# Gate and up of the last feed-forward part as Strassen products in a two-layer trunk kernel on one Trainium2 core

## The chip, the core and the metric

The kernel runs on one core of a Trainium2 chip. The metric is the device time of one execution in microseconds (us); the time of a kernel is the median of several runs. The core has TensorE (matrix products, PE in the profile; its weight loads are PEld), VectorE (DVE), ScalarE (ACT), GpSimd (POOL), SyncE (SP, which issues most of the loads) and 16 DMA engines. Each engine runs its instructions in a fixed order and waits for the others by semaphores.

## What is computed

Two layers over 640 tokens (128 of a context, 512 latent ones) of width 1024. Each layer adds three parts to the residual stream `h`: a feed-forward part, four parallel head groups, and a second feed-forward part. The second feed-forward part of the second layer, with the final norm behind it, ends the program.

```python
def swiglu(x, wg, wu, wd):                       # widths 1024 -> 2816 -> 1024
    return (jax.nn.silu(x @ wg) * (x @ wu)) @ wd

def trunk_layer(h, cond, p, ctx):
    m = modulation(cond, p["w_mod"], p["b_mod"])
    sh1, sc1, g1, sh2, sc2, g2, sh3, sc3, g3 = [m[:, :, j] for j in range(N_MOD)]
    x = rmsnorm(h, p["norm_ffn1"]) * (1 + sc1) + sh1
    h = h + 0.5 * g1 * swiglu(x, p["ffn1_w_gate"], p["ffn1_w_up"], p["ffn1_w_down"])
    x = rmsnorm(h, p["norm_mix"]) * (1 + sc2) + sh2
    mixed, new_ctx = token_mixing(x, p, ctx)
    h = h + g2 * mixed
    x = rmsnorm(h, p["norm_ffn2"]) * (1 + sc3) + sh3
    h = h + 0.5 * g3 * swiglu(x, p["ffn2_w_gate"], p["ffn2_w_up"], p["ffn2_w_down"])
    return h, new_ctx
```

## The kernel before

**Layout.** Activations lie transposed: 8 blocks of 128 features on the partitions, tokens along the free side, in two halves of 256 and 384 tokens. `hT` holds the residual stream. A product at full precision is three matmuls in a rounded format: each operand is kept as a rounded part and a rest (`xh`, `xl` of the activation, `whi`, `wlo` of the weight), and `mm3` (L270 to L278) issues `whi` by `xh`, `whi` by `xl` and `wlo` by `xh`. The hidden width of 2816 is 22 blocks of 128.

**Weights.** SP loads raw slabs of up to 1 MB into a pool of three (`raw`); a slab of gate or up holds two hidden blocks, 1024 by 256. `prep_to` splits each half of a slab: ACT rounds it (`whi`, L220), DVE subtracts (`wlo`, L221). The pairs lie in a ring of six slots; `w` takes the next one and has the split of the two that follow it written ahead.

**The feed-forward part** (`ffn`) works through the hidden blocks in chunks, here 8, 6 and 8. For each block `gate_up` forms gate and up in PSUM, first for the 256 tokens (one tile `gu` for both), then for the 384, 24 matmuls for each product; then ACT does Silu (`sg`, L724), DVE the product with up (`hx`, L726), ACT rounds it (`hh`, L727), DVE takes the rest (`hl`, L728). In the first chunk the first two blocks (`LEAD`) go together, 256 tokens before 384, with the feature blocks in the outer loop (L713 to L715), so that they can begin while the normalised activations are still being made. After a chunk `res_phase` multiplies its `hh` and `hl` by the down weights (`y`, 8 feature blocks by two halves) and adds each result to `hT` on DVE (L642). In the last chunk the last five feature blocks (`FIN`) go half by half, and the final norm and the output of the 384 tokens run beside the products of the 256.

**The activations** come from `x_prep`: `rb` broadcasts the norm's scale by a matmul (L574), DVE scales (`xt`, L599), ACT adds the shift and rounds (`xh`, L602 or L606 and L608), and the rest `xl` is taken on DVE (L603) or on POOL (L609).

**What sets the order.** The program is written as above, and a scheduler that simulates the engines puts the instructions of each engine in their final order when the kernel is built. `tick` counts off the matmul time written so far and writes side work (norms, `x_prep`) in between when it is due.

Of the kernel before, what the change touches and what calls it, by code (L numbers as in the profile page):

```python
# [33 lines left out]
N_TAB = 2  # L34
T_SUM = 2300
# [79 lines left out]
class Net:  # L115
    def __init__(self, tc, a, depth=DEPTH, dump=None):
# [37 lines left out]
        self.x = [None, None]  # L154

# [48 lines left out]
    def prep_to(self, n):  # L204
        while self.i_prep < min(n, len(self.wq), self.limit):
            sid, f = self.wq[self.i_prep]
            self.load_upto(sid + 1)
            v = f(self.raw[sid])
# [13 lines left out]
            self.ready[self.i_prep] = (hv, lv)  # L222
            self.slab_left[sid] -= 1
# [3 lines left out]
            self.i_prep += 1  # L227

# [298 lines left out]
    def load_x(self):  # L527
# [129 lines left out]
    def ffn_specs(self, l, nm, chunks):  # L657
# [21 lines left out]
    def ffn(self, l, j, nxt, chunks, e_pro=None):  # L679
# [4 lines left out]
        nf = max(n for _, n in chunks[:N_TAB if e_pro else None])  # L684
        for ci, (c0, n) in enumerate(chunks):
# [6 lines left out]
            hh = [hp.tile([P, nf, w], F32R, name=f"hh{i}", tag=f"hh{i}") for i, (_, w) in enumerate(HALVES)]  # L692
            hl = [hp.tile([P, nf, w], F32R, name=f"hl{i}", tag=f"hl{i}") for i, (_, w) in enumerate(HALVES)]

            def gate_up(fs, half, wts):
# [12 lines left out]
                if len(fs) > 1:  # L708
                    for k in range(DB):
                        for i, f in enumerate(fs):  # L710
                            for s in range(2):
# [3 lines left out]
                                nc.tensor.matmul(o, wh[:, k, :], xl[:, k, :], start=False, stop=(k == DB - 1))  # L715
                        self.tick(len(fs) * 6 * (w * 0.417 + 2.5))
# [15 lines left out]
            f = 0  # L732
            while f < n:
# [12 lines left out]
        hps.close()  # L746

# [1207 lines left out]
```

## Time and profile before

| | |
|---|---|
| median of 3 runs | 2568.88 us (2568.11 to 2569.06) |
| the profiled execution | 2565.89 us, of which the profile's span 2564.1 us |
| mean granted clock of TensorE | 0.984 of full speed |
| busy TensorE, share of the span | 97%, 17040 instructions |
| the last feed-forward part | from about 2076 us to the end |
| its largest load | 1 MB per slab of two gate or up blocks |

All rows used come from the profiled execution. The page gives busy times over the whole span; the views by stretch, by line and the timeline show one stretch or one engine of it. In a timeline each line is an instruction or a run of like ones: its start, its length, engine and line of the code, the output tile, the inputs, shapes, how many, and in brackets how long the engine had stood idle and what released it. Lengths of matmuls overlap, since they are pipelined; the distance between two starts is the time that one costs.

### The profile page before, as it was taken

The numbers are of one execution on the slowest core, as the hardware profiler recorded it, in microseconds if no ns is written. First come the engines' busy times: TensorE is split into PE (matmuls) and PEld (weight loads), VectorE is DVE, ScalarE is ACT, GpSimd is POOL, SyncE is SP. The second block draws the span as 40 slices with busy tenths as digits, with TensorE's granted clock in tenths as the row PEclk, the third lists the DMA queues.
The fourth block names the chain that finished last, engine by engine and source line by source line (L and its number), as shares of the span: only waits on it lengthen the run. The fifth ranks groups of instructions, "written<-read, shape, count | busy, mean of one in ns | idle before, by whom it ended". The sixth has DMA issues, their size and how long they took to land.

```text
span 2564.1 us, 41328 instructions
## 1 busy us (share of the span) xinstructions
PE 2485.1 (97%) x17040; PEld 2343.6 (91%) x17040; DVE 1518.8 (59%) x3084; ACT 837.0 (33%) x1620; POOL 322.4 (13%) x453
## 2 busy tenths in 40 slices
PE   7999999999899899999999999999998999999998
PEld 5999999997679899999999999999876799999998
DVE  5767676765778678454356666665567773323333
ACT  5332222242454333222243222223435453222222
POOL 2211111036001111000020000000360010000000
PEclk8999999999899999999999999999999999999999
DMA  8545454430204245333314444441301123222211
GB/s 292 168 125 169 132 168 141 130 116 26 59 9 137 71 128 179 105 115 102 98 42 155 133 144 143 135 144 56 114 12 55 42 91 116 66 71 72 89 50 42
DMA packets 209028, 272.08 MB, mean 106 GB/s; under 512 B 25480, under 2 KB 176232, under 8 KB 208584
## 3 DMA queue, kind: packets, MB, share of 16 engines
q1 hardware_dynamic: 186824, 191.45, 23.5%
q0 software_dynamic: 22016, 78.00, 10.2%
q8 instruction: 134, 2.20, 0.3%
q14 instruction: 54, 0.44, 0.1%
HBM read 254.44 MB, written 14.97 MB: 105 GB/s over the span
## 4 chain that ended last, share of the span: by engine, by line
PE 82%; issue 8%; DVE 5%; DMA 2%; POOL 2%; ACT 1%; SPq 0%; DVEq 0%; POOLq 0%; ACTq 0%
PE gu L276 15%; PE gu L278 14%; PE gu L277 14%; PE y L276 8%; PE y L277 8%; PE y L278 8%; PE pj L1055 1%; PE pj L1056 1%; PE pj L1057 1%; PE gu L713 1%; PE gu L714 1%; PE gu L715 1%; PE macc L460 1%; DMA wf<-in_w_mod_dram 1%; DVE xt L599 1%
## 5 line engine op out<-in xcount | busy, mean ns | idle before, releaser
L276 PE MATMUL gu<-xh,whi 128*128 128x384 f32 (+1 forms) x2560 | 792.8, 310 | 0.8 <-ACT whi L220 0.8
L278 PE MATMUL gu<-xh,wlo 128*128 128x384 f32 (+1 forms) x2560 | 788.4, 308 | 0.9 <-DVE wlo L221 0.9
L277 PE MATMUL gu<-xl,whi 128*128 128x384 f32 (+1 forms) x2560 | 788.4, 308 | 0.0
L220 ACT ACTIVATE whi<-raw 128x1024 fp32r<-128x1024 f32 (+2 forms) x344 | 328.4, 960 | 846.7 <-PE gu L277 429.0
L221 DVE TENSOR_TENSOR wlo<-raw,whi 128x1024 fp32r<-128x1024 f32 (+2 forms) x344 | 377.8, 1101 | 340.8 <-ACT whi L220 339.8
L276 PEld LDWEIGHTS gu<-xh,whi 128*128 128x128 f32 x2560 | 480.3, 188 | 11.8 <-issue 10.0
L277 PEld LDWEIGHTS gu<-xl,whi 128*128 128x128 f32 x2560 | 481.3, 188 | 2.7 <-issue 2.4
L278 PEld LDWEIGHTS gu<-xh,wlo 128*128 128x128 f32 x2560 | 480.6, 188 | 2.2 <-DVE wlo L221 1.3
L276 PE MATMUL y<-hh,whi 128*128 128x384 f32 (+1 forms) x1408 | 437.1, 312 | 0.1
L277 PE MATMUL y<-hl,whi 128*128 128x384 f32 (+1 forms) x1408 | 434.4, 309 | 0.0
L278 PE MATMUL y<-hh,wlo 128*128 128x384 f32 (+1 forms) x1408 | 434.4, 309 | 0.0
L642 DVE SCALAR_TENSOR_TENSOR hT<-y,G,hT 128x128 f32<-128x128 f32 (+1 forms) x432 | 175.5, 435 | 216.7 <-PE y L278 215.9
L411 DVE SCALAR_TENSOR_TENSOR mvec<-wm,cs,mvec 128x512 f32<-128x512 f32 x420 | 294.3, 744 | 10.7 <-DMA wm<-in_w_mod_dram 10.5
L276 PEld LDWEIGHTS y<-hh,whi 128*128 128x128 f32 x1408 | 266.6, 190 | 6.7 <-issue 5.8
L278 PEld LDWEIGHTS y<-hh,wlo 128*128 128x128 f32 x1408 | 266.9, 190 | 0.4 <-issue 0.4
L277 PEld LDWEIGHTS y<-hl,whi 128*128 128x128 f32 x1408 | 267.1, 190 | 0.1
L366 POOL DMA_DIRECT2D wm<-in_w_mod_dram x128 | 92.5, 722 | 1039.3 <-DVE mvec L411 794.8
L726 DVE TENSOR_TENSOR hx<-sg,gu 128x256 f32<-128x256 f32 (+1 forms) x176 | 84.8, 483 | 128.7 <-ACT sg L724 128.6
L727 ACT ACTIVATE hh<-hx 128x256 fp32r<-128x256 f32 (+1 forms) x176 | 82.9, 471 | 171.7 <-DVE hx L726 171.5
L724 ACT ACTIVATE sg<-gu 128x256 f32<-128x256 f32 (+1 forms) x176 | 75.4, 429 | 191.3 <-PE gu L278 188.4
L728 DVE TENSOR_TENSOR hl<-hx,hh 128x256 fp32r<-128x256 f32 (+1 forms) x176 | 86.4, 493 | 63.0 <-ACT hh L727 62.9
L561 POOL TENSOR_TENSOR rst<-ms,mhalf 128x2 f32<-128x2 f32 (+1 forms) x12 | 11.2, 932 | 824.3 <-DVE ms L560 824.3
(340 smaller groups left out, 3205.3 us busy)
## 6 DMA issues: line engine op xcount, KB each, us to landing
wm<-in_w_mod_dram POOLq DMA_DIRECT2D x128, 512.0 KB, 4.1
raw<-in_ffn_w_gate_dram SPq DMA_DIRECT2D x44, 1024.0 KB, 5.4
raw<-in_ffn_w_up_dram SPq DMA_DIRECT2D x44, 1024.0 KB, 5.1
raw<-in_ffn_w_down_dram SPq DMA_DIRECT2D x24, 1024.0 KB, 7.2
raw<-in_ffn_w_down_dram SPq DMA_DIRECT2D x16, 768.0 KB, 4.5
raw<-in_w_in_dram SPq DMA_DIRECT2D x12, 1024.0 KB, 5.4
wf<-in_w_mod_dram SPq DMA_DIRECT2D x8, 1024.0 KB, 12.3
raw<-in_ffn_w_down_dram SPq DMA_DIRECT2D x16, 512.0 KB, 5.2
```

Source lines behind the costliest of these rows:

```text
L220: self.nc.scalar.activation(hv, v, AF.Copy)
L221: self.nc.vector.tensor_tensor(lv, v, hv, op=OP.subtract)
L276: self.nc.tensor.matmul(out, wh, xh, start=(i == 0), stop=False)
L277: self.nc.tensor.matmul(out, wh, xl, start=False, stop=False)
L278: self.nc.tensor.matmul(out, wl, xh, start=False, stop=(i == n - 1))
L366: self.nc.gpsimd.dma_start(out=t.rearrange("p (j c) -> p j c", j=2), in_=w[kk * 256:(kk + 1) * 256, c0:c0 + 512].rearrange("(j p) c -> p j ...
L411: nc.vector.scalar_tensor_tensor(self.mvec[:, v], w, c, self.mvec[:, v], op0=OP.mult, op1=OP.add)
L642: self.pin = nc.vector.scalar_tensor_tensor(h, y[:, s:e], G[:, k, v:v + 1], h, op0=OP.mult, op1=OP.add)
L724: nc.scalar.activation(sg[:, 0:w], g, AF.Silu)
L726: nc.vector.tensor_tensor(hx[:, 0:w], sg[:, 0:w], u, op=OP.mult)
L727: nc.scalar.activation(hh[half][:, f, :], hx[:, 0:w], AF.Copy)
L728: self.pin = nc.vector.tensor_tensor(hl[half][:, f, :], hx[:, 0:w], hh[half][:, f, :], op=OP.subtract)
```

## The change

In the last feed-forward part only, the chunks become 2, 4, 4, 4, 4 and 4 blocks, and from the second chunk on two gate blocks, and then two up blocks, are formed together by a Strassen scheme: the slab's 1024 by 256 weights and the 1024 by 640 activations are each cut in two by two, and seven products of half size (512 by 128 weights, 320 tokens, 12 matmuls) take the place of eight.

- `st_x` forms four combinations of the activations at the start of the part, from `xh` + `xl`, on POOL (20 operations) and DVE, splits them again, and writes one of them over a quarter of `xh` and `xl`. It is written in four steps between the matmuls of the first chunk.
- `st_sums` forms the combinations of a slab's weights by four POOL operations of 128 by 512, three of them in place. Instead of two pieces of 1024 columns, a slab is split in four, `A1`, `S24` and `S3` of 1024 columns and `S1` of 512. The split on ACT and DVE (now L232, L233) stays.
- `st_pair` issues the products into three PSUM regions `a`, `b`, `c` (L852 to L854), partly on top of each other. Partial sums that two results need are copied out by ACT (`copy`) and added by DVE. Silu, `hx`, `hh`, `hl` follow with 320 columns.
- The ring has five slots instead of six, from the second layer's output projection on. `xh`, `xl`, `hh`, `hl` are one tile for all 640 tokens each.
- In the Strassen chunks `res_phase` issues the first two feature blocks of down for all but the chunk's last two hidden blocks first (`early`), and those two behind.

The lines below are those of the change, in the order of the file.

```diff
+CHUNKS_S = ((0, 2), (2, 4), (6, 4), (10, 4), (14, 4), (18, 4))
+RING_S = 5
+S1_BUFS = 1
+W_ST = ("A1", "S24", "S1", "S3")
+TH = NTOK // 2
...
+            if f in W_ST:
+                v = self.st_view(sid, raw, f)
+            else:
+                v = f(raw)
...
+            if f == "A1":
+                self.st_sums(sid, raw)
...
+    def st_view(self, sid, raw, f):
+        if f == "S1":
+            return self.s1.pop(sid)
+        return raw[:, :, P:2 * P] if f == "S3" else raw[:, :, 0:P]
+    def st_sums(self, sid, raw):
+        G = self.nc.gpsimd
+        a11, a12 = raw[:, 0:4, 0:P], raw[:, 4:8, 0:P]
+        a21, a22 = raw[:, 0:4, P:2 * P], raw[:, 4:8, P:2 * P]
+        s1 = self.sx.tile([P, 4, P], F32, name="s1", tag="s1", bufs=S1_BUFS)
+        G.tensor_tensor(s1, a21, a22, op=OP.add)
+        G.tensor_tensor(a21, a11, a21, op=OP.subtract)
+        G.tensor_tensor(a11, s1, a11, op=OP.subtract)
+        G.tensor_tensor(a12, a12, a11, op=OP.subtract)
+        self.s1[sid] = s1
...
+        if not self.xt_free:
+            self.xt = [self.xp.tile([P, DB, NTOK], F32R, name=f"x{c}", tag=f"x{c}") for c in "hl"]
+            self.xt_free = [0, 1]
+        self.xt_free.remove(half)
+        c0, w = HALVES[half]
+        return tuple(t[:, :, c0:c0 + w] for t in self.xt)
...
-                    if f % 2 == 0:
+                    if f >= st:
+                        if f % 2 == 0:
+                            self.add_slab(slab(w, f, 2), W_ST)
+                    elif f % 2 == 0:
...
+        if st < FB:
+            e_sx, self.sx = self.open_pool("sx")
+            tprep = self.st_x()
+        else:
+            tprep = iter(())
...
+                        if half == 1 and k % 2:
+                            next(tprep, None)
...
+            if c0 >= st:
+                for f in range(0, n, 2):
+                    self.st_pair(f, hht, hlt)
+                f = n
...
+            for _ in tprep:
+                pass
             last = ci == len(chunks) - 1
-            self.res_phase(n, [(hh[i], hl[i]) for i in range(2)], [(f, f) for f in range(n)], (l, j), nxt if last else None)
+            self.res_phase(n, [(hh[i], hl[i]) for i in range(2)], [(f, f) for f in range(n)], (l, j), nxt if last else None,
+                           early=(n - 2 if c0 >= st else 0))
...
+        def whole(E, k, c):
+            t = self.t(TH, "tr")[:, 0:TH]
+            E.tensor_tensor(t, xh[:, k, c:c + TH], xl[:, k, c:c + TH], op=OP.add)
+            return t
+        def split(E, t, h, lo):
+            A.activation(h, t, AF.Copy)
+            E.tensor_tensor(lo, t, h, op=OP.subtract)
+        for k in range(4):
+            r12, r11, r22 = whole(V, k, TH), whole(V, k, 0), whole(G, 4 + k, TH)
+            t1 = self.sx.tile([P, TH], F32, name="sg", tag="sg", bufs=4)
+            t1s.append(t1)
+            V.tensor_tensor(t1, r12, r11, op=OP.subtract)
+            G.tensor_tensor(r12, r22, r12, op=OP.subtract)
+            split(G, r12, *(t[:, k, TH:NTOK] for t in self.T23))
+            V.tensor_tensor(r22, r22, t1, op=OP.subtract)
+            split(V, r22, *(t[:, k, 0:TH] for t in self.T23))
+            r21 = whole(G, 4 + k, 0)
+            G.tensor_tensor(r21, r21, r22, op=OP.subtract)
+            split(V, r21, *(t[:, k, :] for t in self.T4))
+            yield
+        for k in range(4):
+            split(V, t1s[k], *(t[:, k, TH:NTOK] for t in self.xt))
...
+        X = {"11": [t[:, 0:4, 0:TH] for t in self.xt], "T1": [t[:, 0:4, TH:NTOK] for t in self.xt],
+             "21": [t[:, 4:8, 0:TH] for t in self.xt], "22": [t[:, 4:8, TH:NTOK] for t in self.xt],
+             "T2": [t[:, :, 0:TH] for t in self.T23], "T3": [t[:, :, TH:NTOK] for t in self.T23], "T4": self.T4}
+        def prod(o, w, k0, x, start):
+            (wh, wl), (bh, bl) = w, X[x]
+            for k in range(4):
+                h, lo = wh[:, k0 + k, :], wl[:, k0 + k, :]
+                nc.tensor.matmul(o, h, bh[:, k, :], start=start and k == 0, stop=False, skip_group_check=True)
+                nc.tensor.matmul(o, h, bl[:, k, :], start=False, stop=False, skip_group_check=True)
+                nc.tensor.matmul(o, lo, bh[:, k, :], start=False, stop=(k == 3), skip_group_check=True)
...
+        def copy(o):
+            t = self.t(TH, "cp")[:, 0:TH]
+            A.activation(t, o, AF.Copy)
+            return t
+        sg = {}
+        def gate(i, t, o, part):
+            g = sg[i, t] = self.sx.tile([P, TH], F32, name="sg", tag="sg", bufs=4)
+            if part is not None:
+                V.tensor_tensor(g, o, part, op=OP.add)
+                o = g
+            A.activation(g, o, AF.Silu)
+        def up(i, t, o, part):
+            hx = self.t(TH, "hx")[:, 0:TH]
+            if part is not None:
+                V.tensor_tensor(hx, o, part, op=OP.add)
+                o = hx
+            V.tensor_tensor(hx, o, sg[i, t], op=OP.mult)
+            c = slice(t * TH, t * TH + TH)
+            A.activation(hh[:, f + i, c], hx, AF.Copy)
+            V.tensor_tensor(hl[:, f + i, c], hx, hh[:, f + i, c], op=OP.subtract)
+        for done in (gate, up):
+            ac = self.d2("st")
+            a, c = ac[:, 0, 0:TH], ac[:, 1, 0:TH]
+            b = self.b([P, 512], name="st")[:, 0:TH]
+            w1 = self.w(2)
+            prod(a, w1, 0, "11", True)
+            t1 = copy(a)
+            prod(b, w1, 4, "21", True)
+            done(0, 0, b, t1)
+            w2 = self.w(2)
+            prod(a, w2, 0, "T2", False)
+            u2 = copy(a)
+            w4 = self.w(2)
+            prod(c, w4, 0, "T1", True)
+            t5 = copy(c)
+            w3 = self.w(2)
+            prod(a, w3, 0, "T3", False)
+            done(1, 1, a, t5)
+            prod(c, w2, 4, "22", False)
+            done(0, 1, c, u2)
+            prod(a, w3, 4, "T4", False)
+            done(1, 0, a, None)
...
+        if early:
+            wds = [self.w(1) for _ in range(2)]
+            ys = [(i, half, self.b([P, 512], name="y")) for i in range(2) for half in range(2)]
+            for fs in (order[:early], order[early:]):
+                for i, half, y in ys:
+                    w = HALVES[half][1]
+                    xh, xl = xs[half]
+                    wh, wl = wds[i]
+                    for f, g in fs:
+                        for p, q in ((wh, xh), (wh, xl), (wl, xh)):
+                            nc.tensor.matmul(y[:, 0:w], p[:, f, :], q[:, g, :], start=(f == 0 and p is wh and q is xh),
+                                             stop=(f == n - 1 and p is wl))
+                    self.tick(len(fs) * 3 * (w * 0.417 + 2.5))
+                    if fs[-1] is order[-1]:
+                        self.residual(half, i, y, self.G[G])
+                        if nxt is not None:
+                            self.sq_add(half, i)
+            db = 2
...
+        if l + 1 == self.depth:
+            self.ring_size = RING_S
```

**What moves on the engines.** In the names below a number tells one buffer from another. First DVE, at the start of the last feed-forward part: before, the two products `hx` of the lead blocks with 384 columns stand between weight splits.

```order
L603 SCALAR_TENSOR_TENSOR xl1_20578<-xt_20607,modT1_97,xh1_20577 128x384
L726 TENSOR_TENSOR hx_20666<-sg_20664,gu_20511 128x256
L726 TENSOR_TENSOR hx_20672<-sg_20670,gu_20513 128x256
L728 TENSOR_TENSOR hl0_20495<-hx_20666,hh0_20493 128x256
L728 TENSOR_TENSOR hl0_20495<-hx_20672,hh0_20493 128x256
L221 TENSOR_TENSOR wlo_20799<-raw_20275,whi_20798 128x1024
L726 TENSOR_TENSOR hx_20788<-sg_20786,gu_20688 128x384
```

There each waits only for `sg` and for PSUM, and the first down products follow it. Now, at the same place, the combinations (`tr`, with their split `t23l`, `t4l`) stand ahead of them.

```order
L822 TENSOR_TENSOR t23l_20675<-tr_20768,t23h_20674 128x320
L831 TENSOR_TENSOR tr_20811<-tr_20811,sg_20813 128x320
L822 TENSOR_TENSOR t4l_20677<-tr_20778,t4h_20676 128x320
L822 TENSOR_TENSOR t23l_20675<-tr_20811,t23h_20674 128x320
L774 TENSOR_TENSOR hx_20828<-sg_20826,gu_20648 128x384
L774 TENSOR_TENSOR hx_20834<-sg_20832,gu_20649 128x384
L776 TENSOR_TENSOR hl_20454<-hx_20828,hh_20453 128x384
L776 TENSOR_TENSOR hl_20454<-hx_20834,hh_20453 128x384
```

The two `hx` of 384 columns have moved behind four operations of `st_x` (and more ahead of these). Two of these operations read `tr_20778` and `tr_20811`, which come from POOL, whose order there is now:

```order
L817 TENSOR_TENSOR tr_20778<-xh_20345,xl_20346 128x320
L829 TENSOR_TENSOR tr_20764<-tr_20768,tr_20764 128x320
L817 TENSOR_TENSOR tr_20811<-xh_20345,xl_20346 128x320
L829 TENSOR_TENSOR tr_20807<-tr_20811,tr_20807 128x320
L834 TENSOR_TENSOR tr_20778<-tr_20778,tr_20768 128x320
L822 TENSOR_TENSOR t23l_20675<-tr_20764,t23h_20674 128x320
```

The fifth of these rows, with `tr_20778` in and out, is the sixteenth of the twenty operations of `st_x` on POOL.

TensorE, at the product `rb` that broadcasts the scale of the 384 tokens. Before:

```order
L715 MATMUL gu_20513<-xl0_20389,whi_20507 128x256
L574 MATMUL rb_20573<-diag_20569,ones_73 128x384
L276 MATMUL gu_20806<-xh0_20388,whi_20676 128x256
L277 MATMUL gu_20806<-xl0_20389,whi_20676 128x256
L278 MATMUL gu_20806<-xh0_20388,wlo_20677 128x256
L276 MATMUL gu_20806<-xh0_20388,whi_20676 128x256
```

Now:

```order
L760 MATMUL gu_20477<-xh_20345,wlo_20472 128x256
L761 MATMUL gu_20477<-xl_20346,whi_20471 128x256
L607 MATMUL rb_20537<-diag_20533,ones_73 128x384
L759 MATMUL gu_20648<-xh_20345,whi_20455 128x384
L760 MATMUL gu_20648<-xh_20345,wlo_20456 128x384
L761 MATMUL gu_20648<-xl_20346,whi_20455 128x384
```

Behind `rb` 37 matmuls of a third block have given way to the 384-column products of the lead blocks.

TensorE in the middle of the part, where the up slab of blocks 6 and 7 begins to be finished (`st_21823` is gate, `st_21949` up; `whi_21788` is `S24` of gate, `whi_21951` is `S1` of up, `whi_21858` is `S3` of gate):

```order
L852 MATMUL st_21823<-xh_20345,whi_21788 128x320
L853 MATMUL st_21823<-xl_20346,whi_21788 128x320
L854 MATMUL st_21823<-xh_20345,wlo_21789 128x320
L852 MATMUL st_21949<-xh_20345,whi_21951 128x320
L853 MATMUL st_21949<-xl_20346,whi_21951 128x320
L852 MATMUL st_21823<-t4h_20676,whi_21858 128x320
L853 MATMUL st_21823<-t4l_20677,whi_21858 128x320
```

The first two products with `S1` stand directly behind the last one with the slot's old content. A little later, at the end of this pair (`whi_22136` is `A1` of the next up slab):

```order
L853 MATMUL st_21949<-t4l_20677,whi_21986 128x320
L854 MATMUL st_21949<-t4h_20676,wlo_21987 128x320
L852 MATMUL st_22209<-xh_20345,whi_22136 128x320
L853 MATMUL st_22209<-xl_20346,whi_22136 128x320
L852 MATMUL st_22210<-xh_20345,whi_22136 128x320
L853 MATMUL st_22210<-xl_20346,whi_22136 128x320
L852 MATMUL st_22083<-t23h_20674,whi_22029 128x320
L853 MATMUL st_22083<-t23l_20675,whi_22029 128x320
```

The first products of the next up slab stand directly behind the last of this one, ahead of the next gate slab's (`st_22083`). Before the change, outside the lead blocks, all products of a block stood together, and the next block's behind them.

## Rows read from the trace of the kernel before

**Rows 1.** The page: busy time (share of the span) and instructions of each engine

```profile
PE 2485.1 (97%) x17040; PEld 2343.6 (91%) x17040; DVE 1518.8 (59%) x3084; ACT 837.0 (33%) x1620; POOL 322.4 (13%) x453
```

**Rows 2.** Table by stretch; us, then busy PE, PEld, DVE, ACT, POOL, PEclk, DMA share, GB/s

```profile
2126.00:2202.00 76.00, 76.00 (x517) 76.00 (x515) 25.74 (x35) 22.58 (x34) 0.00 (x0) 1.00 0.30 98
...
2385.00:2497.00 112.00, 112.00 (x771) 112.00 (x770) 34.34 (x49) 30.60 (x48) 0.00 (x0) 1.00 0.21 66
...
2540.00:2564.10 24.10, 17.30 (x134) 16.69 (x132) 8.66 (x22) 6.02 (x11) 0.91 (x2) 0.89 0.27 109
```

**Rows 3.** Timeline of PE in the last feed-forward part; start, us, instruction

```profile
2132.45 0.28 PE L276 MATMUL gu<-xh,whi 128*128 128x256 f32 x1
...
2135.27 0.34 PE L276 MATMUL gu<-xh,whi 128*128 128x384 f32 x1
...
2143.59 0.28 PE L276 MATMUL gu<-xh,whi 128*128 128x256 f32 x1
```

**Rows 4.** Timeline of PE at the start of that part

```profile
2097.46 0.91 PE L574 MATMUL rb<-diag,ones 128*128 128x384 f32 x2 [1.08 <-DVE diag L571]
2097.92 0.57 PE L276 MATMUL gu<-xh,whi 128*128 128x256 f32 x1
...
2102.57 0.34 PE L713 MATMUL gu<-xh,whi 128*128 128x384 f32 x1
```

**Rows 5.** Timeline of POOL there

```profile
2092.04 0.74 POOL L609 TENSOR_TENSOR xl<-xt,xh 128x256 fp32r<-128x256 f32 x1 [2.80 <-ACT xh L608]
...
2101.82 3.97 POOL L609 TENSOR_TENSOR xl<-xt,xh 128x384 fp32r<-128x384 f32 x3 [5.12 <-ACT xh L608]
...
2109.96 1.02 POOL L609 TENSOR_TENSOR xl<-xt,xh 128x384 fp32r<-128x384 f32 x1 [1.57 <-ACT xh L608]
```

**Rows 6.** Timeline of DVE there

```profile
2098.94 2.21 DVE L599 SCALAR_TENSOR_TENSOR xt<-hT,A,rbs 128x384 f32<-128x384 f32 x4 [1.53 <-ACT rbs L576]
2101.06 0.62 DVE L603 SCALAR_TENSOR_TENSOR xl<-xt,modT,xh 128x384 fp32r<-128x384 f32 x1
...
2103.54 3.19 DVE L599 SCALAR_TENSOR_TENSOR xt<-hT,A,rbs 128x384 f32<-128x384 f32 x3
```

**Rows 7.** Groups of ACT from 2000 us on, shapes apart; busy us, mean ns of one

```profile
L220 ACT ACTIVATE whi<-raw 128x1024 fp32r<-128x1024 f32 x60 | 63.5, 1060 | 184.4 <-PE gu L277 96.0 <-PE y L277 79.7 <-PE gu L715 8.0
...
L724 ACT ACTIVATE sg<-gu 128x384 f32<-128x384 f32 x22 | 10.4, 472 | 0.0
...
L220 ACT ACTIVATE whi<-raw 128x512 fp32r<-128x512 f32 x14 | 8.5, 628 | 9.3 <-PE y L277 6.6 <-DMA raw<-in_w_out_dram 2.7
```

**Rows 8.** Groups of DVE from 2000 us on, shapes apart

```profile
L221 DVE TENSOR_TENSOR wlo<-raw,whi 128x1024 fp32r<-128x1024 f32 x60 | 73.4, 1224 | 119.0 <-ACT whi L220 119.0
...
L726 DVE TENSOR_TENSOR hx<-sg,gu 128x384 f32<-128x384 f32 x22 | 12.0, 546 | 0.0
...
L221 DVE TENSOR_TENSOR wlo<-raw,whi 128x512 fp32r<-128x512 f32 x14 | 9.4, 684 | 1.6 <-ACT whi L220 1.6
L726 DVE TENSOR_TENSOR hx<-sg,gu 128x256 f32<-128x256 f32 x22 | 9.3, 421 | 49.5 <-ACT sg L724 49.5
```

**Rows 9.** Timeline of PE at a late split, and at the end of a down product

```profile
2121.53 0.38 PE L278 MATMUL gu<-xh,wlo 128*128 128x256 f32 x1 [0.62 <-DVE wlo L221]
...
2541.90 0.28 PE L276 MATMUL y<-hh,whi 128*128 128x256 f32 x1
```

**Rows 10.** Timeline of DVE at the same two places

```profile
2120.24 1.23 DVE L221 TENSOR_TENSOR wlo<-raw,whi 128x1024 fp32r<-128x1024 f32 x1 [8.65 <-ACT whi L220]
...
2542.10 0.61 DVE L642 SCALAR_TENSOR_TENSOR hT<-y,G,hT 128x128 f32<-128x128 f32 x2 [1.74 <-PE y L278]
```

**Rows 11.** Table by stretch in the first mixer, columns as in rows 2

```profile
674.00:679.40 5.40, 0.15 (x2) 0.02 (x1) 5.37 (x16) 3.21 (x9) 0.00 (x0) 0.89 0.14 49
679.40:688.00 8.60, 8.57 (x34) 6.24 (x35) 8.47 (x22) 4.25 (x10) 0.00 (x0) 0.50 0.10 33
```

**Rows 12.** A group of POOL over the span, shapes apart

```profile
L1186 POOL TENSOR_TENSOR sc<-ee,wscan 128x160 f32<-128x160 f32 x32 | 19.3, 605 | 9.4 <-DVE ee L1112 7.1
```

More of the change, by code (lines that the diff above doesn't have):

```diff
@@ L154, in __init__ @@
         self.x = [None, None]
+        self.xt_free = []
+        self.s1 = {}
+        self.ring_size = RING
     def pool(self, name, bufs=1, **kw):
@@ L530, in load_x @@
         ss = self.per.tile([P, 5], F32, name="ss_in", tag="ss", bufs=2)
-        xin = [self.xp.tile([P, w // P, D], F32, name=f"xin{i}", tag=f"xh{i}") for i, (_, w) in enumerate(HALVES)]
-        junk = self.xp.tile([P, 2, D], F32, name="sqj", tag="xl0")
-        xt = [xin[0][:, i] for i in range(2)] + [xin[1][:, i] for i in range(3)]
+        xin = self.xp.tile([P, 5, D], F32, name="xin", tag="xh")
+        junk = self.xp.tile([P, 2, D], F32, name="sqj", tag="xl")
+        xt = [xin[:, i] for i in range(5)]
         for i in range(5):
@@ L691, in ffn @@
                 nf = max(n for _, n in chunks[N_TAB:])
-            hh = [hp.tile([P, nf, w], F32R, name=f"hh{i}", tag=f"hh{i}") for i, (_, w) in enumerate(HALVES)]
-            hl = [hp.tile([P, nf, w], F32R, name=f"hl{i}", tag=f"hl{i}") for i, (_, w) in enumerate(HALVES)]
+            hht, hlt = (hp.tile([P, nf, NTOK], F32R, name=nm, tag=nm) for nm in ("hh", "hl"))
+            hh, hl = ([t[:, :, h0:h0 + w] for h0, w in HALVES] for t in (hht, hlt))
             def gate_up(fs, half, wts):
@@ L742, in ffn, with st_x @@
                 f += len(grp)
+            for _ in tprep:
+                pass
             last = ci == len(chunks) - 1
-            self.res_phase(n, [(hh[i], hl[i]) for i in range(2)], [(f, f) for f in range(n)], (l, j), nxt if last else None)
+            self.res_phase(n, [(hh[i], hl[i]) for i in range(2)], [(f, f) for f in range(n)], (l, j), nxt if last else None,
+                           early=(n - 2 if c0 >= st else 0))
+        if st < FB:
+            e_sx.close()
         hps.close()
+    def st_x(self):
+        nc = self.nc
+        V, G, A = nc.vector, nc.gpsimd, nc.scalar
+        xh, xl = self.xt
+        self.T23 = [self.sx.tile([P, 4, NTOK], F32R, name=f"t23{c}", tag=f"t23{c}") for c in "hl"]
+        self.T4 = [self.sx.tile([P, 4, TH], F32R, name=f"t4{c}", tag=f"t4{c}") for c in "hl"]
+        t1s = []
+        def whole(E, k, c):
[20 more added lines that the diff above has]
+            split(V, t1s[k], *(t[:, k, TH:NTOK] for t in self.xt))
@@ L1684, in out1, with res_phase @@
                 yield
-    def res_phase(self, n, xs, order, G, nxt, lead=1):
+    def res_phase(self, n, xs, order, G, nxt, lead=1, early=0):
+        nc = self.nc
         def one(db, half, wd):
@@ L1877, in build @@
             n.out_specs(l)
[L1878 removed]
+            if l + 1 < depth:
+                n.ffn_specs(l, "ffn2", CHUNKS4)
+            else:
+                n.ffn_specs(l, "ffn2", CHUNKS_S, CHUNKS_S[1][0])
         n.seg.append((1 << 30, 1 << 30))
@@ L1904, in build @@
                 tab = 0 if l == 0 and j == 0 else (l + 1 if j == 2 and not last else None)
-                chunks = CHUNKS if tab is None else CHUNKS4
+                st = CHUNKS_S[1][0] if last and j == 2 else FB
+                chunks = CHUNKS_S if st < FB else CHUNKS if tab is None else CHUNKS4
                 n.open_modp(2)
@@ L1917, in build @@
                 n.ffn(l, j, (l, 1) if j == 0 else ((None, None) if last else (l + 1, 0)), chunks,
-                      e_pro if tab is not None else None)
+                      e_pro if tab is not None else None, st)
                 n.mod_to(n.m_limit)
```

19 lines of the change are left out of this document (10 added, 9 removed).

## The prediction

> **What bounds the kernel now.** I read the shares of the engines first, then the table by stretch, then the tensor engine's own timeline. TensorE is busy for 97% of the span [rows 1]. In the last feed-forward part it is busy all the time: every microsecond of the two stretches shown, at the full granted clock (1.00, which is 2.4 GHz), while DVE and ACT are busy for about a third of it or less [rows 2]. So there the time is the sum of the matmul steps, and a step is read from starts: 24 matmuls of 256 columns from 2132.45 to 2135.27, 0.1175 us each, then 48 of 384 columns to 2143.59, 0.1733 us each [rows 3]. That is linear in the columns (0.436 ns for one more), so 320 columns should take 0.1454 us.
>
> **The gain.** Two blocks have 96 matmuls of each size: 96 x (0.1175 + 0.1733) = 27.92 us. The Strassen form has 2 x 7 x 12 = 168 of 320 columns: 24.43 us. Ten such pairs save 34.9 us. The down products keep their matmuls. Since nothing hid this work, all of it would be gained if TensorE stayed as full. The rest is what it now waits for. The orders of the engines ahead of this part are the same but for a few neighbours, so I cost that at nothing.
>
> **The start of the part.** (1) Chunk 0 now holds two blocks. In the old order 37 of a third block's 48 matmuls ran between the product that broadcasts the second half's scale (2097.46) and the first 384-column one (2102.57) [rows 4]. Now the 384-column ones follow at once, and need xl, which DVE had at 2101.06 + 0.62 [rows 6]. The scale comes 12 matmuls (1.4 us) earlier, so I take 2 us of wait.
>
> (2) The T operands are made by 20 POOL operations and some 27 of DVE, 320 columns each, and in DVE's order they stand before the two `hx` of 384 columns, which the first down products need. The last thing that DVE must have from POOL before those is its sixteenth operation. POOL begins after its last xl, 2110.98 less 1.4. Alone it takes 0.74 us for 256 columns and 1.02 for 384 [rows 5], so 0.88 for 320 and 14.1 for sixteen. But beside DVE it is slower: three of 384 columns took 3.97 us instead of 3.06 [rows 5], and DVE's three `xt` beside them 3.19 instead of 1.66 [rows 6]. About 5.3 us of work passed in 4.0 there. Sixteen on POOL with 24 on DVE at 0.48 [rows 8] are 25.6 us of work, so 19.3 of time: 2128.9. Then two ACT roundings, Silu, `hx` and `hh`: 2.4 us, 2131.3. TensorE has done its 94 matmuls of 384 columns from 2100.3 on, and six of 256, at 2117.3. It waits 14 us. With no slowing it would be 9, with no overlap at all 22. What is late next, the sums for the first Strassen weights, lies behind 11 us of down products and costs nothing.
>
> (3) After a wait of 5.3 us the granted clock stood at 0.50 (1.2 GHz) for 8.6 us [rows 11]. After 14 idle I take 6 us at half, 3 us lost; 0 to 4.3.
>
> **The ten pairs.** Weights are split on ACT and DVE into a ring of five slots, and a slot is free only when the last product with it has left TensorE. DVE starts 0.20 us after TensorE could go on (2541.90 to 2542.10), and TensorE follows a DVE end by 0.06 (2121.47 to 2121.53) [rows 9, 10]. ACT takes 1.06 us for 1024 and 0.63 for 512 columns, 0.47 for a small one [rows 7]; DVE 1.22, 0.68 and 0.48 between its two sizes [rows 8]. One product of 12 matmuls is 1.74 us. In the new order, per part of four blocks:
> - twice, the first two matmuls with up's S1 stand directly behind the product that frees its slot: 0.20 + 0.63 + 0.06 = 0.89. Together 1.8.
> - once, A1 of the second gate takes the slot that T4 left: 0.20 + 1.06 + 1.22 + 0.06 = 2.54, behind 14 matmuls (2.04): 0.5.
> - once, A1 of the second up stands directly behind up's last product, and on ACT behind `hh` of the result before: 0.20 + 0.48 + 0.68 + 0.48 + 0.47 + 1.06 + 0.06 = 3.43, less one product: 1.7.
> - twice, T2 of up waits for a copy that is behind S3's rounding on ACT: 0.20 + 1.06 + 0.47 + 0.47 + 0.06 = 2.26, less one product: 1.0.
> - at the end, the last `hh` is two results behind, of which six matmuls hide a part: 0.8.
>
> That is 5.8 us, and 29 us for five parts. If only the first kind stays it is 9; if each is also held up by POOL, 41. POOL's four sums per slab (some 5.2 us at 1.3) fit in the 12.2 us that a slab lasts. The two extra rounds of down evacuations per old chunk have DVE time to spare (DVE at 30%).
>
> **The end.** The second half's output had 14 us of down products to hide in, now 7; the stretch after 2540 has 7 us without matmuls [rows 2]. I add 1 us (0 to 3).
>
> **The sum**, on the profiled execution (span 2564.1, time 2565.9): -34.9 + 2 + 14 + 3 + 29 + 1 = +14.1, so 2580.0. The median shown is 3.0 above that execution, so **2583 us**. Two runs of this kernel can be told apart from about 0.2% (5 us).
>
> **The rivals.**
> *The shared reads decide.* Against the forecast's 1.3-fold overlap, DVE operations with two SBUF inputs and POOL's could exclude each other. For it: `xt` took 1.06 instead of 0.55 beside POOL. Against: 5.3 us of work did pass in 4.0. Then (2) costs 22, the clock 4.3, and each part two more microseconds: -34.9 + 2 + 22 + 4.3 + 41 + 1 = +35, 2604. The Trainium skill (SBUF — State Buffer, "Who interferes with whom") says that a DVE instruction with two SBUF inputs contends with a GpSimd one that reads SBUF, and that the loser blocks for the whole instruction. By that rule this rival would hold; the rows agree with the contention, not with all of its size.
>
> *Cheap POOL operations.* A POOL operation of 160 columns took 0.605 us [rows 12]. If 320 cost no more, sixteen take 9.7, the wait is 4.4 and the clock stays: -34.9 + 2 + 4.4 + 29 + 1 = +1.5, 2570, no change. Against it stands the 1.02 of 384. The Trainium skill (GPSIMD Engine Reference, "3.1 Elementwise — side-by-side cycle accounting") gives 4497 ns for an add of 2048 columns; the estimate from it, 0.70 us for 320, would make the wait 6 and the sum some +4. The rows, 0.74 for 256 already, speak against so little.
>
> *The splits come in time* (the other side). Four of the five kinds of wait come from ACT and DVE standing in line, not from the slot. The two engines are under a third busy, and a product that comes late gives them time for the next. If in the gate and up stretches only the slot wait of S1 stays, the parts cost 9: with the lower bounds of the start, -34.9 + 2 + 9 + 1.5 + 9 + 1 = -12.4, 2556; with my own values there 2563. It decides when the waits fall under about 2 us a part. Against it: the order on each engine is fixed, and in the rows TensorE did wait for `wlo` where a split came late [rows 9].
>
> That the change doesn't do what it says I rule out: 240 fewer matmuls stand in TensorE's order.
>
> **How the numbers follow.** Forecast 0.42 (2573 to 2595 with its bounds), shared reads 0.16, cheap POOL 0.18, splits in time 0.24. Slower by over 0.2%: 0.42 + 0.16 = 0.58. Faster: 0.24 and a little of the cheap POOL case, 0.26. Within 0.2%: 0.16. The range goes from the third rival's time to that of the first, 2555 to 2605.
>
> **What would show it.** Right: steps of 0.145 us in the `st` matmuls; a single wait of TensorE of 9 to 16 us for `hh` before the down products of chunk 0, with a lower clock behind it; waits of 0.9 for ACT before S1 of up, and of some 1.7 before the second up's A1, five times each; TensorE busy for some 90% of the gate and up stretches. Wrong: no gap in chunk 0, or parts of four blocks that last 50 us instead of some 55 in gate and up. If TensorE is as full as before, the time is some 30 us lower and the whole argument falls.

## The result: 43.6 us slower

The changed kernel takes 2612.05 us (median of 4 runs, 2610.76 to 2615.05), the kernel before 2568.49 (4 runs, 2563.28 to 2569.06): a ratio of 1.0176, with a 95% interval of 1.0158 to 1.0193. The sign was forecast, the size was not: 2583 was predicted, and the range ended at 2605.

The profiled execution took 2610.76 us. Its page, first the shares of the engines:

```profile
PE 2471.4 (95%) x16800; PEld 2314.1 (89%) x16800; DVE 1656.3 (63%) x3308; ACT 904.7 (35%) x1760; POOL 458.4 (18%) x553
```

TensorE is busy for 14 us less than in [rows 1], but the span is 45 us longer. The table by stretch, columns as in [rows 2], tells where:

```profile
2121.60:2139.40 17.80, 0.14 (x3) 0.01 (x1) 17.40 (x26) 6.57 (x17) 12.97 (x14) 0.63 0.24 74
2139.40:2143.50 4.10, 4.10 (x17) 4.10 (x18) 4.10 (x7) 0.88 (x2) 2.64 (x2) 0.53 0.00 0
...
2255.10:2343.70 88.60, 80.43 (x529) 77.34 (x529) 48.15 (x77) 31.63 (x53) 22.63 (x16) 1.00 0.23 72
```

First comes a hole of 17.8 us before the down products of the first chunk, in which DVE is busy throughout, and 4 us at half clock behind it. Then every four-block part, of which the third row is one, takes 88.6 us with TensorE busy for 80.4. By the steps of [rows 3] such a part is 2 x 24.43 + 27.92 = 76.8 us of matmuls (two pairs and the down products). The waits of TensorE in the last feed-forward part (sum in us, times, longest) name the releasers:

```profile
PE y L309 <- ACT hh L775: 17.7, 1, 17.7
PE st L852 <- DVE hx L874: 14.7, 20, 1.5
PE st L852 <- ACT cp L859: 13.4, 10, 1.4
PE st L852 <- ACT whi L232: 5.8, 10, 0.6
PE st L852 <- DVE hx L876: 5.5, 5, 1.1
```

The part as a whole, from the matmul that broadcasts the scale of the 256 tokens to the end, took 485.7 us before (from 2078.4) and 529.4 now (from 2079.6). Against the steps of [rows 3] this is the sum; a step of 320 columns takes 0.1464 us (eleven steps from 2268.89 to 2270.50 below), where the forecast had 0.1454.

| term | forecast | measured |
|---|---|---|
| fewer matmul steps | -34.9 | -33.2 |
| up to the first down product | +2 | +3.8 |
| wait for `hx` of 384 columns | +14 | +17.8 |
| half clock behind it | +3 | +1.9 |
| ten Strassen pairs | +29 | +55.8 |
| end | +1 | -2.3 |
| sum | +14.1 | +43.8 (the trace: +43.7) |

The 55.8 are what five parts take above the 77.45 us of experiment 1, where the waits of the pairs are gone. So the pairs are mis-sized by 27 us, and the other terms by 3 together.

Of the 3.8 up to the first down product, 1.7 are a lower clock that the forecast did not list there: after waits of 1.9 and 0.9 us for the first `xh` and `xl` of the 384 tokens the steps of 384 columns take 0.32 us for a while.

```profile
2102.40:2105.60 3.20, 3.20 (x10) 3.20 (x11) 3.20 (x4) 1.97 (x5) 3.11 (x3) 0.50 0.00 0
```

At the end TensorE now waits less for the norm than before, and the lower clock that followed that wait (granted 0.51 from 2555.5 to 2559.0 in the kernel before) doesn't come. The waits, before and now:

```profile
PE pss L633 <- DVE sq L625: 1.6, 1, 1.6
PE pss L670 <- ACT yo L2037: 0.4, 1, 0.4
```

**What a pair waits for.** The timeline of TensorE in the second part:

```profile
2268.89 0.31 PE L852 MATMUL st<-t23h,whi 128*128 128x320 f32 x1
...
2270.50 0.31 PE L854 MATMUL st<-t23h,wlo 128*128 128x320 f32 x1
2272.27 0.41 PE L852 MATMUL st<-xh,whi 128*128 128x320 f32 x1 [1.46 <-DVE hx L874]
2272.53 0.31 PE L853 MATMUL st<-xl,whi 128*128 128x320 f32 x1
...
2274.88 0.41 PE L852 MATMUL st<-t4h,whi 128*128 128x320 f32 x1 [0.58 <-DVE hx L874]
```

At 2270.50 is the last matmul of T3 (`t23h`) into `a`. The next product is the one with the activation's quarter 22, into `c`, the next but one T4, into `a`. DVE's timeline there:

```profile
2271.73 0.48 DVE L874 TENSOR_TENSOR hx<-st,cp 128x320 f32<-128x320 f32 x1
...
2274.33 0.49 DVE L874 TENSOR_TENSOR hx<-st,cp 128x320 f32<-128x320 f32 x1 [0.56 <-PE st L854]
```

The first of these reads `a`, and ends at 2272.21; the product into `c` starts 0.06 us later. The second reads `c`, and ends at 2274.82; the product into `a` starts 0.06 later. Each product waits for the reader of the other region. In the code `a` and `c` are the two halves of one tile (`ac`), and by this reading a wait is set for a tile; experiments 1 and 2 test it. The `cp` kind is the same: T3 into `a` waits for the copy of `c`, which stands behind a rounding on ACT. ACT, and TensorE behind it:

```profile
2253.71 1.06 ACT L232 ACTIVATE whi<-raw 128x1024 fp32r<-128x1024 f32 x1 [4.11 <-PE st L853]
2254.68 0.74 ACT L859 ACTIVATE cp<-st 128x320 f32<-128x320 f32 x2
...
2255.15 0.41 PE L852 MATMUL st<-t23h,whi 128*128 128x320 f32 x1 [1.39 <-ACT cp L859]
```

T3 starts 0.06 us after the first of the two copies has ended (they take 0.43 us each). Six of the ten waits of a part are of this sort; the other four are for weight slots (`S1` and `A1`), as forecast, one of them (`hx L876`) for a free PSUM tile as well.

### The profile page after: what moved, and what is told of

Same layout as the page of the kernel before. It is cut to its first block, busy times and chain, and to the rows that moved or that the text cites. A ratio compares the mean times of both kernels' runs of the same rounds, so it can differ in the third digit from the quotient of the medians.

```text
span 2609.0 us, 41506 instructions
## 1 busy us (share of the span) xinstructions
PE 2471.4 (95%) x16800; PEld 2314.1 (89%) x16800; DVE 1656.3 (63%) x3308; ACT 904.7 (35%) x1760; POOL 458.4 (18%) x553
## 4 chain that ended last, share of the span: by engine, by line
PE 82%; DVE 8%; ACT 3%; POOL 3%; DMA 2%; issue 1%; SPq 0%; DVEq 0%; ACTq 0%; POOLq 0%
PE gu L309 11%; PE gu L311 11%; PE gu L310 11%; PE y L309 9%; PE y L310 8%; PE y L311 8%; PE st L852 3%; PE st L853 3%; PE st L854 2%; ACT whi L232 2%; PE O L1771 1%; PE y L1869 1%; DVE wlo L233 1%; PE gu L761 1%; PE gu L759 1%; PE gu L760 1%
## 5 line engine op out<-in xcount | busy, mean ns | idle before, releaser
L232 ACT ACTIVATE whi<-raw 128x1024 fp32r<-128x1024 f32 (+3 forms) x388 | 353.4, 918 | 792.4 <-PE y L310 332.7
L233 DVE TENSOR_TENSOR wlo<-raw,whi 128x1024 fp32r<-128x1024 f32 (+3 forms) x388 | 419.2, 1084 | 293.1 <-ACT whi L232 291.6
L309 PE MATMUL gu<-xh,whi 128*128 128x384 f32 (+1 forms) x1920 | 595.6, 310 | 0.8 <-ACT whi L232 0.8
L310 PE MATMUL gu<-xl,whi 128*128 128x256 f32 (+1 forms) x1920 | 591.5, 308 | 0.0
L311 PE MATMUL gu<-xh,wlo 128*128 128x256 f32 (+1 forms) x1920 | 591.2, 308 | 0.3 <-DVE wlo L233 0.3
L309 PE MATMUL y<-hh,whi 128*128 128x384 f32 (+1 forms) x1328 | 413.9, 313 | 17.7 <-ACT hh L775 17.7
L309 PEld LDWEIGHTS gu<-xh,whi 128*128 128x128 f32 x1920 | 360.2, 188 | 11.7 <-issue 10.0
L310 PEld LDWEIGHTS gu<-xl,whi 128*128 128x128 f32 x1920 | 360.9, 188 | 2.6 <-issue 2.4
L311 PEld LDWEIGHTS gu<-xh,wlo 128*128 128x128 f32 x1920 | 360.4, 188 | 1.3 <-issue 0.8
L679 DVE SCALAR_TENSOR_TENSOR hT<-y,G,hT 128x128 f32<-128x128 f32 (+1 forms) x504 | 203.5, 434 | 166.3 <-PE y L311 161.9
L852 PE MATMUL st<-xh,whi 128*128 128x320 f32 x320 | 100.7, 316 | 20.1 <-DVE hx L874 8.8
```

The source lines that it names most:

```text
L232: self.nc.scalar.activation(hv, v, AF.Copy)
L233: self.nc.vector.tensor_tensor(lv, v, hv, op=OP.subtract)
L309: self.nc.tensor.matmul(out, wh, xh, start=(i == 0), stop=False)
L310: self.nc.tensor.matmul(out, wh, xl, start=False, stop=False)
L311: self.nc.tensor.matmul(out, wl, xh, start=False, stop=(i == n - 1))
L679: self.pin = nc.vector.scalar_tensor_tensor(h, y[:, s:e], G[:, k, v:v + 1], h, op0=OP.mult, op1=OP.add)
```

## The experiments

The time ahead of the last part varied from one profiled execution to the next (its first matmul stood between 2078 and 2088 us), so beside the median I give the part's own length in the profiled execution, from that matmul to the end of the span: 485.7 before, 529.4 changed.

**1. A tile of its own for c.**

```diff
-            ac = self.d2("st")
-            a, c = ac[:, 0, 0:TH], ac[:, 1, 0:TH]
+            a = self.d2("sa")[:, 0, 0:TH]
             b = self.b([P, 512], name="st")[:, 0:TH]
+            c = self.b([P, 512], name="sc")[:, 0:TH]
```

> The edit gives the PSUM region c a tile of its own; a and c were two halves of one tile. Theory (shared tile): TensorE's waits before T3 of gate, before the product with 22 and before T4 of up, 7.1 us in each part of four blocks with their 0.25 us of restart each, are there only because a product into one half waits for the reader of the other half. They go, 36 us in five parts less a few that turn into waits for a weight slot: 2573 to 2585 us. Rival (slow readers): these products wait because DVE and ACT are late with the copies and sums that they need, so they wait as long in two tiles: 2605 to 2615 us.

2557.18 us; against the kernel before 0.9963 (0.9949 to 0.9976), so now a little faster than it. The part takes 474.2 us, 55.2 less than the change as it was. The theory's 36 was too little: all ten waits are gone, those for slots too. The table by stretch of two parts:

```profile
2234.30:2311.80 77.50, 77.50 (x530) 77.35 (x530) 49.54 (x76) 30.73 (x53) 23.23 (x16) 1.00 0.26 82
2311.80:2389.20 77.40, 77.40 (x529) 77.25 (x528) 49.56 (x76) 30.70 (x52) 23.24 (x16) 1.00 0.26 82
```

TensorE is full, and a part takes 77.4 us. With more products free to run, the scheduler puts others ahead of those that need a new slot; that this is why the slot waits went is argued from the new order, not tried by itself.

**2. Sharing the tile otherwise.** The same tiles and banks, but `b` and `c` are now the halves of one tile.

```diff
-            ac = self.d2("st")
-            a, c = ac[:, 0, 0:TH], ac[:, 1, 0:TH]
-            b = self.b([P, 512], name="st")[:, 0:TH]
+            bc = self.d2("st")
+            b, c = bc[:, 0, 0:TH], bc[:, 1, 0:TH]
+            a = self.b([P, 512], name="sa")[:, 0:TH]
```

> The changed kernel with the same PSUM tiles given out otherwise: b and c are now the two halves of one tile, and a has one of its own. Theory (it is a and c in one tile that costs): the products go to a, b, a, c, a, c, a, c, so a and c alternate while b is written once; with a alone nearly all waits of the pairs go, as with two tiles: 2555 to 2564 us. Rival (any two of the three in one tile make the pairs wait, or it was the third buffer that helped): 2580 us or more.

2565.04 us, 1 us over the range; the part takes 479.2 us, 5.0 more than in experiment 1. The view of waits has none left in the pairs. A part of four blocks:

```profile
2270.58:2348.60 78.02, 77.96 (x530) 77.25 (x529) 47.79 (x76) 30.81 (x53) 23.24 (x17) 1.00 0.26 81
```

That is 0.6 us above experiment 1, 3 us in five parts, against the 11.2 a part of the change as it was; the other 2 us lie ahead of the parts, where this execution's clock was low a little longer. So a shared tile costs next to nothing as such: it costs where the products alternate between its halves while other engines read them.

**3. Everything but Strassen.** The new chunks, ring and tiles, all blocks by ordinary products.

```diff
-                n.ffn_specs(l, "ffn2", CHUNKS_S, CHUNKS_S[1][0])
+                n.ffn_specs(l, "ffn2", CHUNKS_S)
...
-                st = CHUNKS_S[1][0] if last and j == 2 else FB
-                chunks = CHUNKS_S if st < FB else CHUNKS if tab is None else CHUNKS4
+                st = FB
+                chunks = CHUNKS_S if last and j == 2 else CHUNKS if tab is None else CHUNKS4
```

> The chunks of 2 and 4 blocks, the ring of five slots, the merged tiles, but all 22 blocks by ordinary products. Theory (the losses are in the Strassen pairs and the combinations): no more than 2 to 9 us above the kernel before, from the shorter filler after the scale's broadcast and the more frequent changes between gate-up and down: 2570 to 2578 us. Rival (chunks and ring): five slots and short chunks make TensorE wait by themselves, 2585 to 2600 us.

2575.35 us, 1.0030 (1.0019 to 1.0042); the part 488.6, 2.9 above before. The losses are not in the chunks or the ring.

**4. No sums of weights.** `st_sums` issues nothing.

```diff
-        G.tensor_tensor(s1, a21, a22, op=OP.add)
-        G.tensor_tensor(a21, a11, a21, op=OP.subtract)
-        G.tensor_tensor(a11, s1, a11, op=OP.subtract)
-        G.tensor_tensor(a12, a12, a11, op=OP.subtract)
-        self.s1[sid] = s1
+        self.s1[sid] = a22
```

> Leaves out the four POOL sums of each weight slab; the four pieces are split from the raw blocks, so gate and up are formed from wrong weights. All orders on TensorE stay. Theory (shared tile): of the waits only the one before the product with 22 of the first up slab shrinks, by 1.2 us in each of five parts, since the split of DVE that stands ahead of the sum it waits for came late behind POOL: 2604 to 2609 us. Rival (shared reads): POOL's sums slow DVE and hold up most of the waits; without them 2585 to 2597 us.

2613.1 us, above the theory's 2604 to 2609; the part 526.2, 3.2 less than with them. The wait before the product with 22 fell from 1.46 to 0.90, and little else moved. The rival, POOL's sums as the cause in the pairs, falls.

**5. Combinations later.** The two lines that make a step of `st_x` between the matmuls of the first chunk are taken out, so all of it is written behind them.

```diff
-                        if half == 1 and k % 2:
-                            next(tprep, None)
```

> The edit writes the combinations of the activations behind the first chunk's matmuls instead of between them, so the hx of 384 columns come ahead of them on DVE. Theory (the 17.7 us wait is DVE's order): TensorE goes on with the down products of the first chunk after some 2.5 us, and the combinations, some 26 us of work, run beside 14 us of down products and the first Strassen products; 2 to 6 us of wait come back there. 2597 to 2604 us. Rival (the combinations as a whole are the bound): the wait only moves to the first product with a combination, 2609 to 2614 us.

2624.23 us, 1.0217 (1.0200 to 1.0233), the part 536.5: slower still, against both. The wait for `hh` falls to 0.65 us, but others take its place:

```profile
PE st L852 <- DVE wlo L233: 6.3, 6, 5.2
PE y L309 <- DVE hT L679: 4.3, 4, 1.9
```

The combinations now stand on DVE among the additions to `hT` and the splits for the first pair, which wait in turn, and the pairs have more of their own waits in this order. In a start that holds only two blocks this move didn't pay.

**6. No combinations**, on top of experiment 1: the products take plain quarters of the activations.

```diff
-            tprep = self.st_x()
+            tprep = iter(())
...
-             "T2": [t[:, :, 0:TH] for t in self.T23], "T3": [t[:, :, TH:NTOK] for t in self.T23], "T4": self.T4}
+             "T2": [t[:, 0:4, 0:TH] for t in self.xt], "T3": [t[:, 4:8, TH:NTOK] for t in self.xt],
+             "T4": [t[:, 4:8, 0:TH] for t in self.xt]}
```

> On top of the two tiles: leaves out the combinations of the activations; the products take plain quarters of the activations instead, so gate and up are wrong. All other work stays. Theory (DVE's order behind the combinations): the 17.6 us wait before the down products of the first chunk falls to the 1 to 2.5 us that the chain Silu, hx, hh takes, and the half clock behind it (2 us) goes: 2536 to 2542 us. Rival (that wait is due to the weights or PSUM of the first chunk): 2550 us or more.

2539.12 us; the part 455.5. The combinations cost 18.7 us of the 474.2, and the wait for `hh` is 0.65 us without them.

**7. Combinations on DVE alone**, on top of experiment 1 (all `G` of `st_x` become `V`).

```diff
-            r12, r11, r22 = whole(V, k, TH), whole(V, k, 0), whole(G, 4 + k, TH)
+            r12, r11, r22 = whole(V, k, TH), whole(V, k, 0), whole(V, 4 + k, TH)
...
-            G.tensor_tensor(r12, r22, r12, op=OP.subtract)
-            split(G, r12, *(t[:, k, TH:NTOK] for t in self.T23))
+            V.tensor_tensor(r12, r22, r12, op=OP.subtract)
+            split(V, r12, *(t[:, k, TH:NTOK] for t in self.T23))
...
-            r21 = whole(G, 4 + k, 0)
-            G.tensor_tensor(r21, r21, r22, op=OP.subtract)
+            r21 = whole(V, 4 + k, 0)
+            V.tensor_tensor(r21, r21, r22, op=OP.subtract)
```

> On top of the two tiles: the twenty POOL operations of the combinations are done by DVE, 47 in all there. Theory (DVE with two SBUF inputs and POOL exclude each other, so that two engines are no faster than one after the other): with 0.48 us for each DVE operation instead of 0.9 to 1.1 for POOL's, hx of 384 columns ends some 5 us sooner, and the wait falls from 17.6 to 11 to 14 us: 2550 to 2554 us. Rival (POOL's share is work that DVE is spared, overlapped 1.3-fold): about as long as now or longer, 2556 to 2563 us.

2552.88 us; the part 467.8, 6.4 less, and the wait 10.7 instead of 17.6. Twenty operations more on DVE make it sooner ready. Why is seen where both work, in the changed kernel's timeline of DVE:

```profile
2118.28 1.16 DVE L822 TENSOR_TENSOR t23l<-tr,t23h 128x320 fp32r<-128x320 f32 x1
2119.36 1.17 DVE L822 TENSOR_TENSOR xl<-sg,xh 128x320 fp32r<-128x320 f32 x1
2120.46 1.16 DVE L817 TENSOR_TENSOR tr<-xh,xl 128x320 f32<-128x320 f32 x1
```

and of POOL:

```profile
2117.97 1.12 POOL L822 TENSOR_TENSOR t23l<-tr,t23h 128x320 fp32r<-128x320 f32 x1
2119.05 1.13 POOL L834 TENSOR_TENSOR tr<-tr 128x320 f32<-128x320 f32 x1
2120.15 1.12 POOL L829 TENSOR_TENSOR tr<-tr 128x320 f32<-128x320 f32 x1
```

Both start one operation every 1.09 us, in step. In this experiment, without POOL, DVE starts one every 0.40:

```profile
2121.40 0.48 DVE L817 TENSOR_TENSOR tr<-xh,xl 128x320 f32<-128x320 f32 x1
2121.80 0.48 DVE L828 TENSOR_TENSOR sg<-tr 128x320 f32<-128x320 f32 x1
2122.20 0.47 DVE L817 TENSOR_TENSOR tr<-xh,xl 128x320 f32<-128x320 f32 x1
```

So in the time in which the two engines do one operation each, DVE alone does 2.7: POOL holds DVE up by more than it takes off it. One after the other the two would take 0.40 and, by the 0.88 that the forecast worked out from [rows 5], 1.28 in all (an estimate); side by side they take 1.09. The Trainium skill (SBUF — State Buffer, "Who interferes with whom") states that a DVE instruction with two SBUF inputs contends with a GpSimd one that reads SBUF, and that whoever comes first has the shared ports for the whole instruction. This trace agrees with the contention (a DVE operation of 1.16 us instead of 0.48); by its 1.09 some of the two operations' time still overlaps, and how much of each is blocked it doesn't show.

**8. Four ordinary blocks first**, on top of experiment 1.

```diff
-CHUNKS_S = ((0, 2), (2, 4), (6, 4), (10, 4), (14, 4), (18, 4))
+CHUNKS_S = ((0, 4), (4, 4), (8, 4), (12, 4), (16, 4), (20, 2))
```

> On top of the two tiles: the first chunk has four ordinary blocks, so 18 instead of 20 blocks are Strassen products. The combinations stand where they were. Theory: one pair less gives back 3.5 us; the matmuls of blocks 2 and 3 can run while the combinations are made, but those with 384 columns need the PSUM tile that hx frees, which stands behind the combinations on DVE, so some 8 us of the 17.6 us wait stay: 2549 to 2556 us. Rival (all of it is covered): 2539 to 2545 us.

2561.36 us, a miss. A part of the wait stays, but as a wait of block 2 for its weights, whose rounding and rest stand behind the combinations on ACT and DVE, and a new one comes at the end:

```profile
PE pss L670 <- DVE sq L662: 7.0, 2, 5.3
PE gu L309 <- ACT whi L232: 4.3, 1, 4.3
PE gu L311 <- DVE wlo L233: 2.5, 1, 2.5
```

The last chunk had become one of two blocks, and its down products no longer cover the norm of the first half.

**9. Steps behind the blocks**, on top of experiment 8, with the combinations on DVE alone as in 7.

```diff
-                        if half == 1 and k % 2:
-                            next(tprep, None)
...
                     gate_up(grp, half, wts)
+                    if len(grp) == 1:
+                        next(tprep, None)
```

> Four ordinary blocks in the first chunk as before it, the combinations all on DVE and written in one step behind each half of blocks 2 and 3, so that every hx comes ahead of the step written after it. Theory: nothing is waited for there any more; against the two tiles alone 17.6 us of wait and 2 us of half clock go, one pair less costs 3.5 us: 2538 to 2545 us. Rival (22 us of DVE work delay hx and the splits of these blocks): 2548 to 2556 us.

2555.34 us, a miss by the same wait at the end, 7 us and some half clock behind it (the part is 469.7 us). The wait for `hh` is gone, and that for a split is 0.6 us. So the time fell into the rival's range, but not by the rival's mechanism.

**10. The short chunk second**, on top of experiment 9.

```diff
-CHUNKS_S = ((0, 4), (4, 4), (8, 4), (12, 4), (16, 4), (20, 2))
+CHUNKS_S = ((0, 4), (4, 2), (6, 4), (10, 4), (14, 4), (18, 4))
```

> Two tiles, four ordinary blocks in the first chunk, all combinations on DVE in steps behind blocks 2 and 3, and the chunk of two blocks is the second instead of the last, so that the last chunk has four blocks of down products to hide the norm. Theory: against the run with the short chunk last (2555 us) the 7 us of wait for the norm of the end and the half clock behind it go: 2543 to 2549 us. Rival (the early short chunk waits for its weights): 2550 us or more.

2541.79 us, 0.9904 (0.9886 to 0.9922), 1 us under the theory's range: 25 us below the kernel before and 70 below the change as it was. The part is 458.6 us. The table by stretch, four parts and more in the first row, the end in the second:

```profile
2180.00:2500.00 320.00, 319.94 (x2179) 318.87 (x2178) 205.89 (x321) 131.81 (x227) 97.24 (x66) 1.00 0.26 82
2500.00:2541.70 41.70, 35.81 (x255) 35.21 (x253) 27.21 (x64) 18.30 (x37) 1.56 (x2) 0.97 0.16 64
```

**11. The same with POOL's share on POOL.**

> As the one before it, but with POOL's twenty operations of the combinations on POOL again. Theory (POOL and two-input DVE operations exclude each other): nothing is gained by the second engine, and hx and the splits of blocks 2 and 3 stand behind sums that wait for POOL; 0 to 8 us above the run with DVE alone: 2546 to 2554 us. Rival (POOL takes work off DVE): 1 to 5 us below it.

2542.97 us (0.9905, 0.9891 to 0.9919), under the theory's 2546 to 2554; the part 458.5 against 458.6. No difference, against theory and rival: where 28 us of matmuls of two ordinary blocks cover the combinations, it doesn't matter which engine makes them.

## Why the prediction was right or wrong

- **The gain** was right but for 1.7 us: 320 columns cost 0.1464 us instead of 0.1454, and with the waits gone a part takes 77.4 us against 76.8 by the working.
- **"The ten pairs"** is the step that failed: 29 us forecast, 55.8 measured. The forecast listed waits for weight slots and for ACT and DVE standing in line. Those for slots were of the size forecast or below (with 0.26 us of stop and restart each: before `S1` 0.84 against 0.89, before the two `A1` together 1.8 a part against 2.2). But six of the ten waits of a part are for the reader of the other half of a shared PSUM tile, and they take 7.2 of its 11.2 us, 36 in five parts; the forecast had none of this kind. One item stands near: T2 of up was to wait for a copy behind S3's rounding, 1.0 us a part, while T3 of gate ran ahead. In the run T3 itself waits for a copy there, of `c`, which it does not need: 3.2 us a part. The waits of the products with 22 and T4 (4.0 us a part) were not listed at all. Experiments 1 and 2 show that which regions share a tile decides nearly all of the 55 us; the slot waits among them went with the order that came of it.
- **The start** was right in kind: one wait for `hh`, half clock behind it. The wait was 17.8 instead of 14, though TensorE came 4.2 us later than forecast (2121.5 instead of 2117.3), since `hh` came 8 us later (2139.3 instead of 2131.3). The overlap was not the fault: at the forecast's prices (0.48 and 0.88) 1.36 us of work passed in 1.09 where both had work, 1.25-fold against 1.3. Three other things were. POOL began 2 us later (2111.72 instead of 2109.6). Its sixteen operations took 21.7 us instead of 19.3, since POOL stood idle for 5.1 of them, released by DVE each time. And behind the sixteenth, which ended at 2133.4, DVE had more in line before `hx` than the 2.4 us allowed; `hh` ended 5.9 us after it. The filler cost 3.8 instead of 2, the clock behind the wait 1.9 instead of 3. That the wait came out within 4 us is in part luck: a late TensorE hid 4 of the 8. The sixteenth operation on POOL, then DVE up to `hx`:

```profile
2132.39 1.04 POOL L834 TENSOR_TENSOR tr<-tr 128x320 f32<-128x320 f32 x1 [0.43 <-DVE tr L831]
...
2134.64 1.14 DVE L822 TENSOR_TENSOR t23l<-tr,t23h 128x320 fp32r<-128x320 f32 x1
2135.71 0.48 DVE L831 TENSOR_TENSOR tr<-tr,sg 128x320 f32<-128x320 f32 x1
2136.11 1.15 DVE L822 TENSOR_TENSOR t4l<-tr,t4h 128x320 fp32r<-128x320 f32 x1
2137.18 1.14 DVE L822 TENSOR_TENSOR t23l<-tr,t23h 128x320 fp32r<-128x320 f32 x1
2138.25 1.20 DVE L774 TENSOR_TENSOR hx<-sg,gu 128x384 f32<-128x384 f32 x2
```

- **The end** was forecast 1 us longer and became 2.3 shorter, as the wait for the norm fell from 1.6 to 0.4 us.
- **Rivals.** "Shared reads" came nearest in time, 2604, and its mechanism holds in part for the combinations: beside POOL a DVE operation takes 1.09 us instead of 0.40, but the wait was 17.8, not its 22 (20.3 by the forecast's own numbers, 25.6 instead of 19.3 of time). For the pairs it falls (experiment 4). "The splits come in time" was wrong for this kernel, but its condition can be made: with the tiles apart the splits are never late. "Cheap POOL" falls: POOL's operations take 0.9 us and more.
- **The range** took the pairs' upper bound, 41, from the same kinds of wait. A kind that was not listed is not bounded so.

## What to carry to other kernels

Before counting on products that accumulate in turn into several PSUM regions, give every region that another engine reads in between a tile of its own: here one shared tile cost 55 us, more than the 33 that fewer matmul steps saved. Where TensorE's order is dense, look for each reader of a region and who writes next into the same tile, not only into the same addresses. Work for DVE and POOL on SBUF operands at the same time gains little from the second engine (here 1.28 us of work in 1.09); put it beside matmuls that are there anyway.

## What the runs showed of the hardware

A stop of TensorE costs some 0.26 us more than the idle time that the view of waits gives: in the timeline above, from 2270.50 to 2272.27 are 1.77 us, of which 0.146 are the step and 1.46 the idle time, and the step behind it takes 0.26 instead of 0.146. After 17.7 us without matmuls TensorE ran at 1.2 GHz (granted 0.53) for 4.1 us, less than the 8.6 of [rows 11] after a shorter wait, and was at 1.00 after that; after waits of 1.9 and 0.9 us at the start of the part it ran at 0.50 for over 3 us.
